# First projection of a two-layer decoder trunk: four row groups, sums seeded into the accumulators, spatial loads a block ahead

## The chip, the cores and the metric

The kernel runs on one core of one Trainium2 chip. The metric is the device time of one execution in microseconds; lower is better. A run's time is the span from the first to the last instruction plus a little around it.

## The reference

A two-layer decoder trunk works on one sequence of 256 tokens with width 2048, all in float32. Each layer takes a conditioning vector c, makes six sections of modulation from it (adaLN), and runs a mixer and a SwiGLU feed-forward (FFN), each behind a modulated RMS norm. The change lies in layer 0, in the projection that feeds its mixer, and in its FFN:

```python
mod = (silu(c) @ ada_w[layer] + ada_b[layer])[:, None, :]
sh_m, sc_m, g_m, sh_f, sc_f, g_f = jnp.split(mod, 6, axis=-1)
hm = rms_norm(x, norm_mix_g[layer]) * (1.0 + sc_m) + sh_m
proj = jnp.einsum('bsd,de->bse', hm, w_in)              # (256, 2048) by (2048, 10272)
u, v, z, xbc, dt_raw = jnp.split(proj, ...)
y_a = chunked_spatial_gating(gelu(u), gelu(v), gm_ln_g, gm_ln_b, gm_w_s, gm_b_s)
y_b = ssd_mixer(z, xbc, dt_raw, ...)                    # conv + silu on xbc, scan, norm, times silu(z)
x = x + (1.0 + g_m) * (concat([y_a, y_b]) @ w_out)
x = x + (1.0 + g_f) * ((silu(hf @ w_gate) * (hf @ w_up)) @ w_down)
```

`chunked_spatial_gating` normalises v over its channels, scales it with gm_ln_g and gm_ln_b, and mixes tokens with a causal 128 by 128 matrix for each of 16 heads (gm_w_s).

## The kernel before

**Products.** A float32 product is made of three products of parts: each operand is split into a high and a low part, and hi by h, lo by h and hi by l are summed. A weight slab of 512 columns and two row tiles (256 of the 2048 input channels) is loaded by SP as `raw` (four buffers), rounded by ScalarE into `hi` (L330, three buffers), and the rest `lo` is made by VectorE (L335, three buffers). `wslab` records these three. An input row tile k is the pair `h`, `l`: ScalarE makes h from the normalised x and the modulation (L529), VectorE makes l (L530).

**Blocks and accumulators.** The projection is done in blocks of 512 output columns, 14 of them in the part that the change touches, in the order of `ORDER`: x (the convolution's input, transposed), v and z. x and z blocks come from `dense_ws`, whose weight is the moving operand (12 products of 256 columns for each row tile), v blocks from `dense_as` (6 products of 512 columns for each row tile). A block's sum stands in one of two PSUM accumulators of 128x1024 (`psA`, named accps). The pool gives a block the accumulator that was released first, in the order in which the program asks for them.

**Row groups.** The contraction cannot run over all 16 row tiles at once, since each row tile needs its piece of sh_m and sc_m, and these come from ada_w (a stream of `araw` loads, accumulated on VectorE at L205 and L207, then transposed on PE at L153, reduced at L220, added to the bias at L224). So `grouped` splits the 16 row tiles into `GROUPS`, here of 4, 5 and 7. For each group it runs all 14 blocks over the group's row tiles. After the first group, ScalarE copies the accumulator into an SBUF buffer (L584). In the later groups VectorE adds the accumulator to that buffer (L586). While a group runs, the modulation of the next (a `group_unit`) is loaded and accumulated in the background; `RATES` says how many such steps are put between slabs, `LAGS` how late their VectorE part follows. The first group has no cover: `opening` waits for its modulation, loaded right after x, with some matmuls on the landed tiles that only keep PE warm (`firsts`).

**Last group.** After a block of the last group, `finish0` takes its full sum from the SBUF buffer: convolution and silu for x, gelu with a running sum for v (L987), silu for z (L990). After the tenth block comes the LayerNorm of v, and at the blocks in `GM_AT` one quarter of v is normalised (L952) and mixed (L960, L962), with the loads of gm_ln_g, gm_ln_b and gm_w_s issued at that place.

**Order.** A scheduling layer sets the order of each engine from the order of recording and from priorities (`high_priority`, `issue_after`). Each engine then runs its list in that order, and waits on semaphores.

The FFN of layer 0 uses the same `grouped` with two groups of eight row tiles (`FGROUPS`) and 12 blocks.

Of the kernel before, what the change touches and what calls it, by code (L numbers as in the profile page):

```python
# [39 lines left out]
FIRST_A = (7, 8, 9)  # L40
SMALLS_AT = 4
QUIET = 8
RATES = (1.3, 0.92, 0.0)
RATE = 0.75
# [4 lines left out]
LN_AT = 9  # L49
GM_AT = (9, 11, 12, 13)  # L50
SSD_AT = (12, 14, 18, 20)
# [3 lines left out]
def trunk(ctx: ExitStack, tc: tile.TileContext, x, c, norm_mix_g, norm_ffn_g, ada_w, ada_b,  # L55
# [59 lines left out]
    first_rows = {8: lambda: nc.sync.dma_start(rows3[0:96, :], ada_b[0].rearrange("(k p) -> k p", p=P)),  # L115
                  9: lambda: nc.sync.dma_start(rows3[96:128, :], norm_mix_g.rearrange("l (k p) -> (l k) p", p=P))}

# [72 lines left out]
    def ada_unit(layer, base, stride, width, dst, nr=2):  # L190
# [18 lines left out]
        def end():  # L209
            n = width // P  # L210
            if nr == 1:
                first_mod.append(acc)
                return
            total = tmp.tile([P, 32], F32, tag="tot", name="tot", bufs=2)[:, 0:nr * n]
# [12 lines left out]
            if dst[0][0] in (2, 5):  # L227
                gate_to_rows(layer, dst[0][0])

        for g0 in range(0, KT * nr, nk):  # L230
            raw = (bt() if nr == 1 and g0 not in FIRST_A else
                   adp.tile([P, 1024], F32, tag="araw", name="araw", bufs=A_BUFS))
            for i in range(nk):
# [143 lines left out]

    def dense_ws(w, c0, ks, ahead=W_AHEAD):

        acc = psA.tile([P, 1024], F32, tag="acc", name="accps").rearrange("p (n t) -> p n t", n=4)  # L380
        done = 0
        for run in slabs(ks):
# [12 lines left out]
            for n, (a, b, first, final) in order:  # L395
                dense_mm[0] = T.matmul(acc[:, n, :], a[:, n * P:(n + 1) * P], b, start=first and n % 2 == 0,  # L396
                                       stop=final, skip_group_check=True)
# [18 lines left out]

    def dense_as(w, c0, ks, ahead=W_AHEAD, head=None, tail=False, hold=False):

        if tail:
            accs = [pm(), pm()]
        else:
            full = psA.tile([P, 1024], F32, tag="acc", name="accps").rearrange("p (n t) -> p n t", n=2)
            accs = [full[:, 0, :], full[:, 1, :]]
# [5 lines left out]
        for pi, part in enumerate(parts):  # L431
# [15 lines left out]
            for n, j, (r, i, x) in order:  # L447
# [7 lines left out]
                def product(n=n, j=j, i=i, x=x, bh=bh, bl=bl, hi=hi, lo=lo, last=pi == len(parts) - 1):  # L455
                    return mm(accs[n], (bl if x == 1 else bh)[:, n * P:(n + 1) * P], (lo if x == 2 else hi)[:, i, :],
                              first=pi == 0 and j == 0, last=last and j == len(ops) - 1)

# [88 lines left out]

    def grouped(blocks, groups, layer, sh, make, finish, rates, lags, heads=None, early=0):

# [3 lines left out]
        def begin(gi):  # L553
# [6 lines left out]
            hs.extend(make(k0, kg))  # L560

        for gi, (k0, kg) in enumerate(groups):
            if not (early and gi):
# [4 lines left out]
            for i, (dense, w, c0, dst) in enumerate(blocks):  # L568
                if early and not last and i == len(blocks) - early:
                    begin(gi + 1)  # L570
                args = {"head": heads} if heads and gi == 0 and i == 0 else {}
                if not ks:
# [5 lines left out]
                if dst is None:  # L578
                    if gi == 0:
                        fdst.append(tb())  # L580
                    dst = fdst[i]
                with tc.high_priority(offset=600):
                    if gi == 0:
                        A.activation(dst, acc, AF.Copy)  # L584
                    else:
                        V.tensor_tensor(dst, acc, dst, op=OP.add)  # L586
                if last:
                    finish(i)
                if gi == 0 and sh == 0 and i == 10:
                    later_cols()  # L590
# [5 lines left out]
    with tc.high_priority(offset=50000):  # L596
# [40 lines left out]
        with tc.issue_after(last.ins):  # L637
            psw = pm()
            for t in firsts[10:]:
                mm(psw, ident, t)  # L640
        take()

    def opening(w, c0, n):
# [67 lines left out]

        acc = psA.tile([P, 1024], F32, tag="acc", name="accps").rearrange("p (n t) -> p n t", n=4)

# [219 lines left out]
    def layer_norm():  # L933
# [9 lines left out]
        V.reciprocal(rv, rv)  # L943

    def layer_norm_apply(b):
        gB = t2()
        nc.sync.dma_start(gB, gm_ln_g[:, 512 * b:512 * (b + 1)].partition_broadcast(P))
        bB = t2()
        nc.sync.dma_start(bB, gm_ln_b[:, 512 * b:512 * (b + 1)].partition_broadcast(P))
        for cc in range(2):  # L950
# [4 lines left out]
    def spatial(b):  # L955
        wraw = t2().rearrange("p (h s) -> p h s", h=4)
        nc.sync.dma_start(wraw, gm_w_s[0, 4 * b:4 * b + 4].rearrange("h t s -> t h s"))
        ps = pm()
        for h in range(4):
            T.transpose(ps[:, h * P:(h + 1) * P], wraw[:, h, :], ident)  # L960
        w = t2().rearrange("p (h t) -> p h t", h=4)
# [15 lines left out]

    def finish0(i):
        kind, j = (ORDER[i][0], int(ORDER[i][1])) if i < len(ORDER) else ("", 0)
# [4 lines left out]
        elif kind == "v":  # L984
            t = vt[j]
            for cc in range(2):
                A.activation(t[:, cc, :], t[:, cc, :], AF.Gelu_apprx_tanh, accum_out=sums[:, cc, j:j + 1])  # L987
        elif kind == "z":
            with tc.high_priority(offset=600):
                A.activation(zb[j], zb[j], AF.Silu)  # L990
# [312 lines left out]

    def finishf(i):
        t = fdst[i]
        with tc.high_priority(offset=600):
            if i % 2 == 0:
                A.activation(t, t, AF.Silu)
            else:
                sg = fdst[i - 1]  # L1310
                V.tensor_tensor(sg, t, sg, op=OP.mult)
                ffn_split(sg, 4 * (i // 2), a)

    hf = grouped(fblocks, FGROUPS, 0, 3, makef, finishf, F_RATES, (LAGS[-1], LAGS[-1]), normf.head, 2)
    ffn_in(0, hf, 4 * FPAIRS, 6 - FPAIRS, a)
# [197 lines left out]
```

## Time and profile before

| | us |
|---|---|
| median of 3 runs | 2564.55 |
| lowest, highest | 2564.42, 2566.23 |
| profiled execution, its time | 2565.73 |
| its span, first to last instruction | 2563.9 |
| PE busy in the span | 2528.8 |
| VectorE (DVE) busy | 1862.2 |
| ScalarE (ACT) busy | 1265.6 |
| first product of the first block | 37.79 |
| first product of the second group | 121.69 |

The profile is one execution. The engines are PE (matmul), PEld (its weight loads), DVE (VectorE), ACT (ScalarE), POOL (GpSimd) and SP (which issues most DMAs). A row of a timeline has the start, the duration, the engine, the line in the kernel, the operation, and output and input by their names; what stands in brackets is the idle time before it and what ended that. A group row has the count, then the busy time, the mean in nanoseconds and the idle time. A windows row has, for each engine, the busy time and count, then the clock that PE was granted (1.00 is full speed), the share of time that the DMA engines were busy, and what they moved in GB/s. The projection up to the end of its last group takes the first 393 us.

### The profile page before, as it was taken

How to read it: one execution, taken by the hardware profiler on the slowest of the kernel's cores; microseconds unless marked ns; L12 is line 12 of the kernel's file. 1: busy time of each engine (PE TensorE's matmuls, PEld its weight loads, DVE VectorE, ACT ScalarE, POOL GpSimd, SP SyncE). 2: the span in 40 equal slices, each digit the busy share in tenths (PEclk: the TensorE clock that was granted, in tenths of full speed). 3: DMA queues.
4: the chain of work that ended last, by engine and by line, in shares of the span. 5: the costliest groups of instructions: out<-in, count | busy, mean ns of one | idle time of the engine just before them, and what ended most of it. 6: DMA issues, size and time to landing. Idle time of an engine off the chain costs nothing.

```text
span 2563.9 us, 33519 instructions
## 1 busy us (share of the span) xinstructions
PE 2528.8 (99%) x12485; PEld 2128.0 (83%) x12485; DVE 1862.2 (73%) x1993; ACT 1265.6 (49%) x1640; POOL 6.5 (0%) x19
## 2 busy tenths in 40 slices
PE   7999989999999999999999999999999999999999
PEld 6999888878788888888888788888788888888887
DVE  6799888899878888777777777677764455545454
ACT  5534766555545444344444665554744443344443
POOL 0000000000000000000000000000000000000000
PEclk9999999999999999999999999999999999999999
DMA  8999668998799989999988688878676656666664
GB/s 325 321 343 328 185 202 259 309 318 297 264 326 329 314 302 310 325 316 302 302 308 304 223 282 261 272 263 282 197 257 196 192 189 200 204 190 189 188 204 166
DMA packets 309630, 676.01 MB, mean 264 GB/s; under 512 B 24272, under 2 KB 26842, under 8 KB 309466
## 3 DMA queue, kind: packets, MB, share of 16 engines
q1 hardware_dynamic: 309338, 673.85, 79.2%
q8 instruction: 98, 1.61, 0.2%
q14 instruction: 66, 0.54, 0.1%
q10 hardware_dynamic: 128, 0.02, 0.0%
HBM read 671.62 MB, written 2.16 MB: 263 GB/s over the span
## 4 chain that ended last, share of the span: by engine, by line
PE 96%; DVE 1%; DMA 1%; ACT 1%; issue 0%; SPq 0%; DVEq 0%; ACTq 0%
PE accps L162 79%; PE accps L396 8%; PE pm L162 6%; PE pm L153 2%; DMA t<-in_gm_w_s 1%; DVE acc L207 0%; DMA blk<-in_ada_w 0%; ACT hi L330 0%; DVE lo L335 0%; DMA raw<-in_ffn_w_gate 0%; DVE t L867 0%; PE pm L887 0%; ACT t L939 0%; DVE t L1145 0%; ACT h L1141 0%
## 5 line engine op out<-in xcount | busy, mean ns | idle before, releaser
L330 ACT ACTIVATE hi<-raw 128x1024 fp32r<-128x1024 f32 (+1 forms) x864 | 903.6, 1047 | 1177.1 <-PE accps L162 1016.8
L335 DVE TENSOR_TENSOR lo<-raw,hi 128x1024 fp32r<-128x1024 f32 (+1 forms) x864 | 1040.3, 1206 | 578.1 <-ACT hi L330 571.4
L162 PE MATMUL accps<-hi,h 128*128 128x512 f32 x2224 | 603.8, 392 | 0.0
L162 PE MATMUL accps<-lo,h 128*128 128x512 f32 x2224 | 600.4, 391 | 0.0
L162 PE MATMUL accps<-hi,l 128*128 128x512 f32 x2224 | 599.9, 390 | 0.0
L162 PEld LDWEIGHTS accps<-hi,l 128*128 128x128 f32 x2224 | 416.5, 188 | 87.1 <-issue 0.8
L162 PEld LDWEIGHTS accps<-lo,h 128*128 128x128 f32 x2224 | 415.4, 188 | 87.1 <-issue 1.6
L162 PEld LDWEIGHTS accps<-hi,h 128*128 128x128 f32 x2224 | 412.6, 188 | 83.3 <-issue 0.6
L207 DVE SCALAR_TENSOR_TENSOR acc<-araw,ct,acc 128x1024 f32<-128x1024 f32 (+2 forms) x377 | 465.3, 1234 | 2.7 <-DMA araw<-in_ada_w 2.0
L162 PE MATMUL accps<-hi,blk 128*128 128x512 f32 x1440 | 357.4, 390 | 0.0
L162 PEld LDWEIGHTS accps<-hi,blk 128*128 128x128 f32 x1440 | 269.5, 188 | 55.5
L162 PE MATMUL accps<-lo,blk 128*128 128x512 f32 x720 | 192.6, 389 | 0.0
L396 PE MATMUL accps<-h,lo 128*128 128x256 f32 x624 | 164.0, 287 | 3.1 <-DVE lo L335 3.1
L396 PE MATMUL accps<-h,hi 128*128 128x256 f32 x624 | 163.7, 286 | 2.3 <-ACT h L529 1.7
L396 PE MATMUL accps<-l,hi 128*128 128x256 f32 x624 | 163.2, 286 | 0.4 <-DVE l L530 0.4
L162 PEld LDWEIGHTS accps<-lo,blk 128*128 128x128 f32 x720 | 135.1, 188 | 28.0
L396 PEld LDWEIGHTS accps<-h,hi 128*128 128x128 f32 x624 | 115.2, 193 | 4.5 <-ACT h L529 1.9
L396 PEld LDWEIGHTS accps<-h,lo 128*128 128x128 f32 x624 | 114.7, 194 | 4.7 <-DVE lo L335 3.5
L396 PEld LDWEIGHTS accps<-l,hi 128*128 128x128 f32 x624 | 115.0, 195 | 0.8 <-DVE l L530 0.6
L162 PE MATMUL pm<-hi,blk 128*128 128x512 f32 x224 | 57.0, 390 | 0.6 <-ACT hi L330 0.6
L586 DVE TENSOR_TENSOR blk<-accps,blk 128x1024 f32<-128x1024 f32 x40 | 48.7, 1218 | 3.8 <-PE accps L162 2.6
L162 PEld LDWEIGHTS pm<-hi,blk 128*128 128x128 f32 x224 | 42.0, 188 | 9.8 <-ACT hi L330 1.1
(277 smaller groups left out, 1319.4 us busy)
## 6 DMA issues: line engine op xcount, KB each, us to landing
araw<-in_ada_w SPq DMA_DIRECT2D x323, 512.0 KB, 5.6
raw<-in_ffn_w_gate SPq DMA_DIRECT2D x176, 512.0 KB, 4.5
raw<-in_ffn_w_up SPq DMA_DIRECT2D x176, 512.0 KB, 4.5
raw<-in_ffn_w_down SPq DMA_DIRECT2D x176, 512.0 KB, 4.4
raw<-in_ab_w_in SPq DMA_DIRECT2D x128, 512.0 KB, 5.0
raw<-in_cd_w_in SPq DMA_DIRECT2D x96, 512.0 KB, 4.7
raw<-in_ab_w_out SPq DMA_DIRECT2D x64, 512.0 KB, 5.5
raw<-in_cd_w_out SPq DMA_DIRECT2D x32, 512.0 KB, 5.0
```

Source lines behind the costliest of these rows:

```text
L153: return T.transpose(dst, src, ident)
L162: return T.matmul(o, a, b, start=first, stop=last, skip_group_check=True)
L207: V.scalar_tensor_tensor(acc, r, ct[nr][:, g:g + 1], acc, op0=OP.mult, op1=OP.add)
L330: A.activation(hi, raw, AF.Copy)
L335: wlast[1] = V.tensor_tensor(lo, raw, hi.bitcast(F32), op=OP.subtract)
L396: dense_mm[0] = T.matmul(acc[:, n, :], a[:, n * P:(n + 1) * P], b, start=first and n % 2 == 0, stop=final, skip_group_check=True)
L586: V.tensor_tensor(dst, acc, dst, op=OP.add)
```

## The change

There are three edits. First, `GROUPS` becomes four groups of 2, 3, 5 and 6 row tiles. Second, in the inner groups, and for v and z blocks of the last group, ScalarE writes a block's running sum into the accumulator before the block's first product (in the rows below: `accps<-blk`, a seed; its block's products then only add). The copy-out after a block is then ScalarE's in all groups but the last, and `finish0` reads v and z straight out of the accumulator. x blocks of the last group still start from zero and are added by VectorE. A function `reserve` takes the accumulators of the present block and of the next one. Third, `load_gm` issues the LayerNorm and spatial loads of a quarter one block before they are used, into tiles of their own. The same seeds serve the FFN of layer 0, where both kinds of block are read from the accumulator. Lines in the changed kernel stand up to some 40 lower or higher than before (hi L328, lo L333, seed L580, copy-out L610, h L531, gelu L1022).

```diff
-GROUPS = ((0, 4), (4, 5), (9, 7))
+GROUPS = ((0, 2), (2, 3), (5, 5), (10, 6))
-LAGS = (2, 4, 6)
+LAGS = (2, 2, 4, 6)
-RATES = (1.3, 0.92, 0.0)
+RATES = (1.3, 1.3, 0.92, 0.0)
-GM_AT = (9, 11, 12, 13)
+GM_AT = (9, 11, 13, 15)
...
-                dense_mm[0] = T.matmul(acc[:, n, :], a[:, n * P:(n + 1) * P], b, start=first and n % 2 == 0,
+                dense_mm[0] = T.matmul(acc[:, n, :], a[:, n * P:(n + 1) * P], b, start=first and n % 2 == 0 and not seeded,
...
+        def seeded(gi, i):
+            return gi > 0 and (gi < len(groups) - 1 or direct(i))
+
+        def reserve(at):
+
+            n = order.index(at)
+            for gi, i in order[n:n + 2]:
+                if (gi, i) not in accs:
+                    accs[gi, i] = acc_tile()
+                    if seeded(gi, i):
+                        dst = blocks[i][3] if blocks[i][3] is not None else fdst[i]
+                        with tc.high_priority(offset=600):
+                            A.activation(accs[gi, i], dst.rearrange("p n t -> p (n t)"), AF.Copy)
+            return {"into": accs[at], "seeded": seeded(*at)}
...
+                if last and direct(i):
+                    finish(i, acc)
+                    continue
                 with tc.high_priority(offset=600):
-                    if gi == 0:
+                    if not last:
                         A.activation(dst, acc, AF.Copy)
                     else:
                         V.tensor_tensor(dst, acc, dst, op=OP.add)
...
-            for t in firsts[10:]:
+            for t in firsts[4:]:
...
+    def load_gm(b):
+        t = gm_loads[b] = [tmp.tile([P, 512], F32, tag="gate", name="gm", bufs=2) for _ in range(2)]
+        t += [tmp.tile([P, S], F32, tag="wg", name="wg", bufs=1), hp.tile([P, S], F32, tag="l%d" % KT, name="wg")]
+        with tc.issue_after(wlast[0].ins):
+            nc.sync.dma_start(t[0], gm_ln_g[:, 512 * b:512 * (b + 1)].partition_broadcast(P))
...
-            for cc in range(2):
-                A.activation(t[:, cc, :], t[:, cc, :], AF.Gelu_apprx_tanh, accum_out=sums[:, cc, j:j + 1])
+            with tc.high_priority(offset=600):
+                for cc in range(2):
+                    A.activation(t[:, cc, :], acc[:, cc, :], AF.Gelu_apprx_tanh, accum_out=sums[:, cc, j:j + 1])
         elif kind == "z":
             with tc.high_priority(offset=600):
-                A.activation(zb[j], zb[j], AF.Silu)
+                A.activation(zb[j], acc, AF.Silu)
...
         for b in range(4):
+            if GM_AT[b] == i + 1:
+                load_gm(b)
...
-    grouped(blocks0, GROUPS, 0, 0, make0, finish0, RATES, LAGS)
+    grouped(blocks0, GROUPS, 0, 0, make0, finish0, RATES, LAGS, lambda i: ORDER[i][0] != "x")
```

How the change stands on the engines is shown at three places. The numbers behind the names are those of the tiles.

The first is ScalarE in the last group, from the slabs of block x5 (the third of `ORDER`) to the gelu of v0 (the second) and beyond. Before:

```order
L330 ACTIVATE hi_2842<-raw_2840 128x1024
L330 ACTIVATE hi_2872<-raw_2870 128x1024
L821 ACTIVATE t2_2584<-t2_2584 128x64
L822 ACTIVATE t2_2584<-t2_2584 128x64
L330 ACTIVATE hi_2902<-raw_2900 128x1024
L330 ACTIVATE hi_2932<-raw_2930 128x512
L987 ACT_TABLE_LOAD
L987 ACTIVATE blk_316,sums_330<-blk_316 128x512 x2
L330 ACTIVATE hi_2976<-raw_2974 128x1024
```

Now (accps_2988 is v0's accumulator, accps_3166 that of v1, the fourth block; hi_3170, 3200 and 3230 are x5's slabs):

```order
L328 ACTIVATE hi_3170<-raw_3168 128x1024
L580 ACTIVATE accps_3166<-blk_307 128x1024
L328 ACTIVATE hi_3200<-raw_3198 128x1024
L328 ACTIVATE hi_3230<-raw_3228 128x1024
L1022 ACT_TABLE_LOAD
L1022 ACTIVATE blk_306,sums_320<-accps_2988 128x512 x2
L328 ACTIVATE hi_3286<-raw_3284 128x1024
```

The gelu, which read and wrote an SBUF buffer behind VectorE's add, now reads the accumulator; the seed of v1 has come in two slabs ahead of it. The accumulator of x5 between them, accps_3106, has the same PSUM address as accps_2988, and its first product waits for the second gelu. The same holds for the blocks behind v1, v2, v3 and z0.

The second is PE around the end of the first group. Before (h_431 is group 0's last row tile, h_1323 group 1's first):

```order
L396 MATMUL accps<-l_432,hi 128x256
L153 MATMUL pm<-ident,acc 128x128 x5
L396 MATMUL accps<-h_431,lo 128x256
L396 MATMUL accps<-h_431,hi 128x256
...
L396 MATMUL accps<-h_431,lo 128x256
L396 MATMUL accps<-h_1323,hi 128x256 x4
L396 MATMUL accps<-h_1323,lo 128x256 x4
```

Now (h_368 is group 0's last, h_876 and h_882 group 1's first two; the L161 rows are block v0's):

```order
L398 MATMUL accps<-h_368,lo 128x256
L152 MATMUL pm<-ident,acc 128x128 x3
L398 MATMUL accps<-h_876,hi 128x256 x4
L398 MATMUL accps<-h_876,lo 128x256 x4
L161 MATMUL accps<-hi,h_876 128x512 x2
L161 MATMUL accps<-hi,h_882 128x512 x2
L398 MATMUL accps<-l_877,hi 128x256 x4
```

The transposes of the next group's modulation stood ten products before the group's end and stand behind its last product now. Products of the second block have come in between those of the first.

The third is ScalarE behind that place, in the first three blocks of group 1 (accps_836, accps_892 and accps_952 in turn; hi_956 is the second block's slab, hi_1067 the fourth's):

```order
L531 ACTIVATE h3_882<-xs3_230,mod0_0_113,gs_0_1_2_872 128x256
L328 ACTIVATE hi_930<-raw_928 128x512
L328 ACTIVATE hi_956<-raw_954 128x1024
L531 ACTIVATE h4_888<-xs4_237,mod0_0_113,gs_0_1_2_872 128x256
L328 ACTIVATE hi_977<-raw_975 128x512
L328 ACTIVATE hi_996<-raw_994 128x1024
L328 ACTIVATE hi_1031<-raw_1029 128x512
L610 ACTIVATE blk_304<-accps_836 128x1024
L328 ACTIVATE hi_1067<-raw_1065 128x1024
L610 ACTIVATE blk_306<-accps_892 128x1024
L580 ACTIVATE accps_952<-blk_305 128x1024
```

The copy-outs L610 and the seed L580 are new in this group, where VectorE's add L586 stood; the third block's seed stands behind the fourth block's hi and the second block's copy-out.

More of the change, by code (lines that the diff above doesn't have):

```diff
@@ L213, in end @@
                 return
[L214 removed]
+            total = t1()[:, 0:nr * n]
             for j0 in range(0, n, 4):
@@ L230, in ada_unit @@
         for g0 in range(0, KT * nr, nk):
-            raw = (bt() if nr == 1 and g0 not in FIRST_A else
-                   adp.tile([P, 1024], F32, tag="araw", name="araw", bufs=A_BUFS))
+            raw = bt() if nr == 1 else adp.tile([P, 1024], F32, tag="araw", name="araw", bufs=A_BUFS)
             for i in range(nk):
@@ L376, in queue_turns, with acc_tile, dense_ws @@
             preps.append(lambda j=j: turn(j, src[j // 2], make))
-    def dense_ws(w, c0, ks, ahead=W_AHEAD):
-        acc = psA.tile([P, 1024], F32, tag="acc", name="accps").rearrange("p (n t) -> p n t", n=4)
+    def acc_tile():
+        return psA.tile([P, 1024], F32, tag="acc", name="accps")
+    def dense_ws(w, c0, ks, ahead=W_AHEAD, into=None, seeded=False):
+        acc = (into or acc_tile()).rearrange("p (n t) -> p n t", n=4)
         done = 0
@@ L415, in run_held, with dense_as @@
                 dense_mm[0] = held.pop(0)()
-    def dense_as(w, c0, ks, ahead=W_AHEAD, head=None, tail=False, hold=False):
+    def dense_as(w, c0, ks, ahead=W_AHEAD, head=None, tail=False, hold=False, into=None, seeded=False):
         if tail:
@@ L423, in dense_as @@
         else:
-            full = psA.tile([P, 1024], F32, tag="acc", name="accps").rearrange("p (n t) -> p n t", n=2)
+            full = (into or acc_tile()).rearrange("p (n t) -> p n t", n=2)
             accs = [full[:, 0, :], full[:, 1, :]]
@@ L456, in product @@
                     return mm(accs[n], (bl if x == 1 else bh)[:, n * P:(n + 1) * P], (lo if x == 2 else hi)[:, i, :],
-                              first=pi == 0 and j == 0, last=last and j == len(ops) - 1)
+                              first=pi == 0 and j == 0 and not seeded, last=last and j == len(ops) - 1)
                 if hold and len(part) > 1 and n == 1 and j >= len(ops) - 2:
@@ L546, in trunk, with grouped @@
     fdst = []
-    def grouped(blocks, groups, layer, sh, make, finish, rates, lags, heads=None, early=0):
+    def grouped(blocks, groups, layer, sh, make, finish, rates, lags, direct, heads=None, early=0):
         hs = []
@@ L560, in begin @@
             hs.extend(make(k0, kg))
+        order = [(gi, i) for gi in range(len(groups)) for i in range(len(blocks))]
+        accs = {}
+        def seeded(gi, i):
[10 more added lines that the diff above has]
+            return {"into": accs[at], "seeded": seeded(*at)}
         for gi, (k0, kg) in enumerate(groups):
@@ L570, in grouped @@
                     begin(gi + 1)
-                args = {"head": heads} if heads and gi == 0 and i == 0 else {}
+                args = reserve((gi, i)) if ks else {}
+                if heads and gi == 0 and i == 0:
+                    args["head"] = heads
                 if not ks:
@@ L588, in grouped @@
                     finish(i)
-                if gi == 0 and sh == 0 and i == 10:
+                if gi == 1 and sh == 0 and i == 2:
                     later_cols()
@@ L710, in rest @@
                 run("V", lambda: V.scalar_tensor_tensor(h[k][1], xs[k], g[k], t, op0=OP.mult, op1=OP.subtract))
-        acc = psA.tile([P, 1024], F32, tag="acc", name="accps").rearrange("p (n t) -> p n t", n=4)
+        acc = acc_tile().rearrange("p (n t) -> p n t", n=4)
         def products(k):
@@ L943, in layer_norm @@
         V.reciprocal(rv, rv)
+    gm_loads = {}
+    def load_gm(b):
[3 more added lines that the diff above has]
+            nc.sync.dma_start(t[0], gm_ln_g[:, 512 * b:512 * (b + 1)].partition_broadcast(P))
+            nc.sync.dma_start(t[1], gm_ln_b[:, 512 * b:512 * (b + 1)].partition_broadcast(P))
+            for i in range(2):
+                nc.sync.dma_start(t[2 + i].rearrange("p (h s) -> p h s", h=2),
+                                  gm_w_s[0, 4 * b + 2 * i:4 * b + 2 * i + 2].rearrange("h t s -> t h s"))
     def layer_norm_apply(b):
[L946 to L949, printed above, removed]
+        gB, bB = gm_loads[b][0:2]
         for cc in range(2):
@@ L976, in ssd_out, with finish0 @@
             ssqy.add(zb[g][:, j, :])
-    def finish0(i):
+    def finish0(i, acc=None):
         kind, j = (ORDER[i][0], int(ORDER[i][1])) if i < len(ORDER) else ("", 0)
```

20 lines of the change are left out of this document (9 added, 11 removed).

## The prediction

> **What bounds the kernel now.** I read the page's head and chain first, then a table of windows over the stage that the change touches, then the timelines at its seams. Page: the span, the engines' busy time, the chain by engine.
>
> ```profile
> span 2563.9 us, 33519 instructions
> PE 2528.8 (99%) x12485; PEld 2128.0 (83%) x12485; DVE 1862.2 (73%) x1993; ACT 1265.6 (49%) x1640; POOL 6.5 (0%) x19
> PE 96%; DVE 1%; DMA 1%; ACT 1%; issue 0%; SPq 0%; DVEq 0%; ACTq 0%
> ```
>
> PE is the bound: 35.1 us of the span (2563.9 - 2528.8) are not matmul. The change removes no dense product, so it can only move those 35 us, or the time lost to a lower clock, which counts as busy. Windows (busy per engine, then PE clock, DMA share, GB/s):
>
> ```profile
> 10.00:30.00 20.00, 14.40 (x75) 11.56 (x75) 16.30 (x18) 8.34 (x24) 0.00 (x0) 1.00 1.05 406
> 35.00:40.00 5.00, 5.00 (x25) 5.00 (x25) 2.48 (x10) 1.97 (x4) 0.00 (x0) 0.50 0.42 117
> 120.00:122.00 2.00, 0.31 (x2) 0.31 (x3) 1.91 (x3) 1.98 (x3) 0.00 (x0) 1.00 0.95 379
> 124.00:126.00 2.00, 2.00 (x11) 2.00 (x11) 2.00 (x5) 1.08 (x3) 0.00 (x0) 0.50 0.72 260
> 130.00:222.00 92.00, 92.00 (x662) 87.18 (x661) 87.26 (x90) 38.06 (x43) 0.00 (x0) 1.00 0.97 340
> 222.00:393.00 171.00, 163.70 (x1187) 152.62 (x1186) 145.39 (x232) 115.82 (x192) 0.00 (x0) 0.99 0.72 223
> 330.00:333.00 3.00, 3.00 (x28) 3.00 (x27) 2.55 (x6) 1.79 (x5) 0.00 (x0) 1.00 0.87 295
> 339.00:342.00 3.00, 3.00 (x16) 3.00 (x16) 3.00 (x5) 0.47 (x2) 0.00 (x0) 0.52 0.76 208
> 393.00:2560.00 2167.00, 2162.75 (x9912) 1786.66 (x9910) 1532.05 (x1554) 1044.06 (x1300) 4.95 (x6) 1.00 0.79 261
> ```
>
> After 393 us PE idles 4.3 us in 2167: nothing to win there. In 130 to 222 DVE is 95% busy and DMA share 0.97, yet PE never waits, so relieving DVE there is worth nothing. What can move is the opening, the seams between groups, and the last group (222 to 393), which idles 7.3 us. PE's waits in that window, PE's timeline at the opening and the first seam, and two pieces of the chain:
>
> ```profile
> PE pm L960 <- DMA t<-in_gm_w_s: 3.6, 2, 2.3
> PE accps L396 <- DVE lo L335: 3.1, 2, 2.4
> ```
> ```profile
> 25.45 3.82 PE L162 MATMUL pm<-blk,ident 128*128 128x512 f32 x8
> 34.53 3.50 PE L162 MATMUL pm<-ones,acc 128*128 128x64 f32 x16 [2.63 <-DVE acc L207]
> 37.79 1.20 PE L162 MATMUL accps<-h,hi 128*128 128x256 f32 x4
> 45.26 1.09 PE L162 MATMUL accps<-hi,h 128*128 128x512 f32 x4
> 118.06 0.71 PE L153 MATMUL pm<-ident,acc 128*128 128x128 f32 x5
> 121.69 0.74 PE L396 MATMUL accps<-h,hi 128*128 128x256 f32 x4 [1.74 <-ACT h L529]
> 123.28 1.11 PE L396 MATMUL accps<-l,hi 128*128 128x256 f32 x4 [0.37 <-DVE l L530]
> ```
> ```profile
> 3.12 8.06 DMA blk<-in_ada_w
> 62.11 5.75 PE accps L396 x48
> ```
>
> Durations for the sum, from the groups of 0 to 400 us:
>
> ```profile
> L330 ACT ACTIVATE hi<-raw 128x1024 fp32r<-128x1024 f32 x101 | 106.7, 1058 | 117.8 <-PE accps L396 70.4 <-PE accps L162 26.8 <-DMA raw<-in_ab_w_in 13.5
> L584 ACT ACTIVATE blk<-accps 128x1024 f32<-128x1024 f32 x14 | 14.1, 1010 | 7.5 <-PE accps L396 4.4 <-PE accps L162 3.1
> L586 DVE TENSOR_TENSOR blk<-accps,blk 128x1024 f32<-128x1024 f32 x28 | 34.1, 1217 | 0.7 <-PE accps L396 0.7
> L207 DVE SCALAR_TENSOR_TENSOR acc<-araw,ct,acc 128x640 f32<-128x640 f32 x31 | 27.3, 881 | 1.3 <-DMA araw<-in_ada_w 1.0
> L207 DVE SCALAR_TENSOR_TENSOR acc<-araw,ct,acc 128x1024 f32<-128x1024 f32 x17 | 21.6, 1273 | 0.1
> L987 ACT ACTIVATE blk<-blk 128x512 f32<-128x512 f32 x8 | 5.0, 625 | 0.7 <-DVE blk L586 0.7
> L987 ACT ACT_TABLE_LOAD x3 | 3.8, 1283 | 0.1
> L990 ACT ACTIVATE blk<-blk 128x1024 f32<-128x1024 f32 x3 | 3.1, 1049 | 1.0 <-DVE blk L586 1.0
> L529 ACT ACTIVATE h<-xs,mod,gs 128x256 fp32r<-128x256 f32 x12 | 6.3, 588 | 0.0
> ```
>
> **The change, part by part.** *Opening.* Two row tiles instead of four halve the first adaLN accumulation: 16 updates of 512 columns instead of 16 of 1024, and 4.2 MB instead of 8.4 MB at the 406 GB/s of 10 to 30 us (10 us less of loading). From 0.881 at 640 columns and 1.273 at 1024, one of 512 takes about 0.75; the first data lands at 11.2, so DVE, with its small steps between, ends near 26. PE's own work is then last: at 25.45 its earlier products are done, eight warming matmuls (3.82, the row of 25.45) end at 29.3, the sums halve (3.50/2 = 1.75), so the first product starts near 30.9, 6.9 earlier than 37.79. There is no 2.63 us hole before it, so the half clock of 35 to 40 goes too. The first block took 45.26 - 37.79 = 7.47 us; twelve-matmul blocks later take 5.75 for 48 matmuls (0.12 each), so 1.7 were lost. **-8.6.**
>
> *Spatial loads a block ahead.* The 3.6 us on the spatial weights go, and so do the 3.1 us on lo, which stands on DVE behind the LayerNorm step that waits for its own loads. The 1.4 us of clock lost in 339 to 342 (3 us at 0.52) and 0.3 around it go with them. On SP the loads now stand among the weight slabs of the block before, 0.77 MB (three of 256 KB) in some 9 us at DMA share 0.72, in one issue more per block since the spatial weights come in halves: free. **-8.4.**
>
> *Seam 0 to 1.* In the order, unit 1's transposes stand behind all of group 0's products; before, ten products followed them. The chain of 118.06 to 121.69 (3.63 us: transposes, reduce, two updates of mod, gs, h) becomes about 3.6 after the last product, since a three-row reduce is shorter but one more update of 640 columns stands ahead of mod. Then block 1's hi stands on ACT behind both h and one other hi (0.59 + 0.6 for half a slab + 1.06, against 0.96 us of products): 1.1 more. Block 2's seed stands behind a hi that needs the end of block 1, and behind block 1's copy-out: from 0.5 before block 1's end, 1.06 + 1.01 + 1.05 (seed) + 0.1, so 2.7. Sum 7.4 against some 2.8 idle now (3.63 less ten products at 0.12, plus the 0.37 ahead of 123.28): **+4.6.** Bounds: 0, if PE's queue absorbs both, and +8, if DMA cannot hold the pace of group 0.
>
> *The seed's price* is not in the trace. ACT moving 1024 columns costs 1.010 out of the accumulator and 1.058 between buffers; I take 1.05, range 1.0 to 1.1. It removes a DVE add of 1.217 in 22 of 28 blocks, worth nothing, since DVE ends no wait there.
>
> *Seams 1 to 2 and 2 to 3, and seeds inside group 1.* Per three-row block ACT now has 1.06 + 0.63 + 1.01 + 1.05 = 3.75 of 4.3 us (36 products at 0.12). At the next seam five h (0.588 each) and the seed follow a copy-out on ACT, and the first product waits for the seed: an estimate of +1.5, since half of that queue already stands there today; six h at the last: +0.7; seeds that stand behind a hi inside the group: +0.9. **+3.1** (0 to 6). Group 0's last block gets the same accumulator as the one before it, and waits for the copy-out: **+1.1.**
>
> *Last group.* This carries the sum. Before, blocks alternated between two accumulators, so an epilogue always had a block's time. Now the seed of the next v or z block takes the free one early, and the x block between gets the accumulator that the v block has just left. It cannot start until both gelus have read it. On ACT ahead of them stands the x block's third hi, whose buffer the v block's last slab holds. Timeline of ACT and PE at such a place now:
>
> ```profile
> 268.22 0.62 PE L162 MATMUL accps<-hi,l 128*128 128x512 f32 x2
> 269.13 0.64 PE L396 MATMUL accps<-h,hi 128*128 128x256 f32 x4
> ```
> ```profile
> 268.88 1.06 ACT L330 ACTIVATE hi<-raw 128x1024 fp32r<-128x1024 f32 x1 [0.75 <-PE accps L162]
> 270.65 0.63 ACT L987 ACTIVATE blk<-blk 128x512 f32<-128x512 f32 x1 [0.71 <-DVE blk L586]
> 271.28 0.61 ACT L987 ACTIVATE blk<-blk 128x512 f32<-128x512 f32 x1
> 280.30 1.28 ACT L840 ACT_TABLE_LOAD   x1
> 281.59 0.23 ACT L840 ACTIVATE dte<-dte 128x32 f32<-128x32 f32 x1
> ```
>
> hi begins when the last hi-by-l product ends (268.84). With a two-row last slab, four more products of 0.23 follow, so the next block would start 0.7 after that. From there hi 1.06, table load 1.28, gelus 0.63 + 0.61, and 0.1 for the accumulators' read-out: 3.7. PE stands 3.7 - 0.7 = 3.0, four times: 12.0. The block after z0 waits likewise for hi and silu, 1.06 + 1.05 + 0.2 = 2.3. Behind the gelus on ACT stand the hi of the block after and the convolution's steps; they have a block's time and are not late. **+14.3** (10 if the hi or the load is early, 16 if the hi is late by half its time each).
>
> Here a rule bears. In the rows, 280.30 + 1.28 runs straight into the next instruction at 281.59, so a switch costs 1.28. The Trainium skill, "ScalarE: Activation LUTs", section "What ACT_TABLE_LOAD costs", adds a drain of about 1380 ns to every switch; by it the four places would cost an estimated 5.5 more. The trace shows none, and the sum goes by the trace.
>
> *Clock.* After 1.7 us of idle in 120 to 122 PE ran at 0.50 in 124 to 126; after 2.3 us in 327 to 330 it kept 1.00. So each new stall of 2.7 to 3.0 us costs 0 to 1.7 more; half, five times: **+4.2.** The Trainium skill, "TensorE: Matmul & The Clock Gate", section "What's actually happening", halves the clock after an idle window of about 3.4 us; by it 3.0 us stalls cost nothing here. The trace has the loss after less idle, so I keep the half.
>
> *FFN.* Same edit in two groups. DVE adds (12) become seeds; PE has no wait there to remove. The last block of its first group shares an accumulator and waits for one copy-out: **+1.1.**
>
> Sum: -8.6 - 8.4 + 4.6 + 3.1 + 1.1 + 14.3 + 4.2 + 1.1 = +11.4. The profiled execution took 2565.73, 1.83 around its span and 1.2 above the median of the three runs, so 2577.1 against it, and 2576 as a median.
>
> **Rivals.** *Faster:* ACT runs ahead of where I put it, so that its hi, table load and seeds are done when PE needs them, and only what needs a finished sum stays on the path. For it: ACT is busy 68% of 222 to 393 (115.82 of 171) and 41% of 130 to 222. Against: the hi ahead of the gelus needs a buffer that the v block holds almost to its end. Then the gelu pair costs 1.3, four times 5.2, silu 1.1, the clock nothing, group 1's seeds and block 2's wait nothing: 11.4 - 8.0 - 4.2 - 3.1 - 2.7 = -6.6, so 2558. It decides where the last group's waits stay under 2 us each.
>
> *No change:* the gelu waits come as forecast, but the clock holds and PE's queue fills the first seam: 11.4 - 4.2 - 4.6 = +2.6, so 2567.
>
> *DMA-bound:* groups 0 to 2 now load ten row tiles of weights (14 blocks of 0.26 MB each, 36.7 MB), adaLN for all 16 (4.2 + 29.4), 16 steps of later sections (8.4) and x (2.1): 81 MB by the start of the last group near 243 us, 333 GB/s on average. The trace held 340 at share 0.97 in 130 to 222 without a stall, and 406 at the opening. If 340 is the ceiling with the opening's slow start, 0 to 10 us more: up to 2586.
>
> **How the numbers follow.** A difference under 0.2% (5.1 us) is no change here. Forecast as summed 0.5, DMA-bound 0.2, no change 0.18, faster 0.12. Below 2559.4: 0.12; within: 0.18; above 2569.7: 0.70. Low end 2560: clock 0, seams at their low bounds. High end 2593: DMA 10, clock and seams at their high bounds in part. The range is set by the clock (0 to 8), the seams (0 to 14) and the gelu waits (10 to 16).
>
> **What would show it.** Right: the first product near 31 us at clock 1.0; no wait on in_gm_w_s; five waits of accps for the gelu or silu in the last group, 2 to 3 us each, and a clock below 1 after them; one wait of the third block of group 1 for the seed; the last group ending near 405. Wrong: no wait on gelu, which removes 14 us; or waits on raw<-in_ab_w_in in the first 240 us, which would mean DMA.

## The result, and the profile after

The changed kernel takes 2590.97 us (median of 4 runs, 2588.35 to 2593.67) against 2564.49 us before (2564.17 to 2566.23): a ratio of 1.0103, 95% interval 1.0087 to 1.0119. It is slower, by 26.5 us where 11.4 were forecast. The profiled execution is the fastest of the four, 2588.35 us, and that of before (2565.73) one of its slower ones, so the traces compare at +22.6 and can't show where the other 3.9 us of the 26.5 lie. Each experiment below is given as its median, then the ratio to the kernel before with its 95% interval. All medians of the experiments below stand beside runs of the kernel before on the same chip, which gave 2563.2 to 2564.0.

The page of the changed kernel, the lines that answer to those shown of before:

```profile
span 2586.6 us, 33665 instructions
...
PE 2529.8 (98%) x12475; PEld 2127.1 (82%) x12475; DVE 1833.3 (71%) x1995; ACT 1343.6 (52%) x1720; POOL 4.9 (0%) x19
...
PE 84%; ACT 2%; DMA 1%; DVE 1%; issue 0%; SPq 0%; ACTq 0%; DVEq 0%
```

PE's busy time is the same within 1 us (2528.8 before). So 21.7 of the 22.7 us of span are idle time of PE (time at a low clock counts as busy). VectorE has lost 29 us of work, ScalarE has gained 78. PE's waits, the largest, of the whole span (total, times, longest in us; left out are those of the opening that stood in the kernel before too):

```profile
PE accps L398 <- ACT blk L1022: 11.7, 4, 4.7
...
PE accps L398 <- ACT accps L580: 5.3, 3, 3.3
...
PE accps L398 <- ACT h L531: 3.3, 1, 3.3
PE accps L398 <- ACT blk L1025: 2.8, 1, 2.8
...
PE accps L398 <- DVE lo L333: 2.4, 4, 1.0
PE pm L152 <- DVE acc L206: 2.2, 1, 2.2
...
PE pm L161 <- DVE t L937: 1.8, 1, 1.8
PE accps L398 <- ACT blk L610: 1.1, 1, 1.1
```

L1022 is the gelu, L1025 the silu, L580 the seed. PE's timeline shows where they fall: the first product, the seam from group 0 to 1, the third block of group 1, group 2's first, the start of the last group (250.43), its five waits, and its end:

```profile
29.74 0.74 PE L161 MATMUL accps<-h,hi 128*128 128x256 f32 x4 [0.69 <-ACT h L725]
...
67.99 0.74 PE L398 MATMUL accps<-h,hi 128*128 128x256 f32 x4 [1.11 <-ACT blk L610]
...
73.31 0.55 PE L152 MATMUL pm<-ident,acc 128*128 128x128 f32 x3 [2.19 <-DVE acc L206]
...
77.21 1.22 PE L398 MATMUL accps<-h,hi 128*128 128x256 f32 x4 [3.35 <-ACT h L531]
...
90.88 1.22 PE L398 MATMUL accps<-h,hi 128*128 128x256 f32 x4 [3.29 <-ACT accps L580]
...
148.03 0.74 PE L398 MATMUL accps<-h,hi 128*128 128x256 f32 x4 [1.71 <-ACT accps L580]
...
250.43 0.28 PE L156 MATMUL pm<-h,t 128*32 128x256 f32 x1
...
276.11 0.73 PE L398 MATMUL accps<-h,hi 128*128 128x256 f32 x4 [2.82 <-ACT blk L1022]
...
299.20 1.22 PE L398 MATMUL accps<-h,hi 128*128 128x256 f32 x4 [4.70 <-ACT blk L1022]
...
320.54 0.74 PE L398 MATMUL accps<-h,hi 128*128 128x256 f32 x4 [2.82 <-ACT blk L1022]
...
340.44 1.22 PE L398 MATMUL accps<-h,hi 128*128 128x256 f32 x4 [1.31 <-ACT blk L1022]
...
362.09 0.74 PE L398 MATMUL accps<-h,hi 128*128 128x256 f32 x4 [2.80 <-ACT blk L1025]
...
414.71 1.17 PE L161 MATMUL accps<-hi,h 128*128 128x512 f32 x4
```

Of before, the start and the end of the last group:

```profile
222.74 0.28 PE L157 MATMUL pm<-h,t 128*32 128x256 f32 x1
...
393.11 1.08 PE L162 MATMUL accps<-hi,h 128*128 128x512 f32 x4
```

The stage ends 21.6 us later (414.71 - 393.11), so nearly all is lost before 415 us. A row tile of the 14 blocks takes 19.8 us (10 times 12 products at 0.12, 4 times 6 at 0.227). The last group has one row tile less, so it would have started at 222.74 + 19.8 = 242.5 with the old losses. It starts at 250.43: the regrouping has cost 7.9 by then, though the first product is 8.05 earlier. The last group takes 164.3 us; 170.4 - 19.8 = 150.6 would be the old figure, so it has lost 13.7. The five waits are 14.5 us. PE's other waits there, for the scan's outputs most of all, are 4.0 us, where all waits of the last group were 7.3 before; a lower clock (0.97 for 0.99) is most of the rest. What stands behind the last group adds 1.1 us (0.7 of them the wait in the FFN for a copy-out, forecast as 1.1).

ScalarE ahead of the first of the five waits reads as it was foreseen:

```profile
272.41 1.06 ACT L328 ACTIVATE hi<-raw 128x1024 fp32r<-128x1024 f32 x1 [1.61 <-PE accps L161]
273.49 1.28 ACT L1022 ACT_TABLE_LOAD   x1
274.79 0.60 ACT L1022 ACTIVATE blk<-accps 128x512 f32<-128x512 f32 x1
...
275.37 0.59 ACT L1022 ACTIVATE blk<-accps 128x512 f32<-128x512 f32 x1
```

hi, table load, two gelus, and PE goes on at 276.11. Ahead of the second of them (4.70, PE idle from 294.50) the convolution's steps of the block before, with a table load of their own, stand ahead of that hi:

```profile
291.36 1.28 ACT L895 ACT_TABLE_LOAD   x1
...
294.24 1.07 ACT L890 ACTIVATE t<-blk,cols 128x256 f32<-128x256 f32 x2
...
295.52 1.04 ACT L328 ACTIVATE hi<-raw 128x1024 fp32r<-128x1024 f32 x1
```

### The profile page after: what moved, and what is told of

It reads as the page before. It is cut to its first block, busy times and chain, and to the rows that moved or that the text cites. A ratio compares the mean times of both kernels' runs of the same rounds, so it can differ in the third digit from the quotient of the medians.

```text
span 2586.6 us, 33665 instructions
## 1 busy us (share of the span) xinstructions
PE 2529.8 (98%) x12475; PEld 2127.1 (82%) x12475; DVE 1833.3 (71%) x1995; ACT 1343.6 (52%) x1720; POOL 4.9 (0%) x19
## 4 chain that ended last, share of the span: by engine, by line
PE 84%; ACT 2%; DMA 1%; DVE 1%; issue 0%; SPq 0%; ACTq 0%; DVEq 0%
PE accps L161 75%; PE pm L161 5%; PE pm L152 2%; PE accps L398 1%; ACT hi L328 0%; DMA wg<-in_gm_w_s 0%; DVE lo L333 0%; ACT L895 0%; DMA raw<-in_ffn_w_gate 0%; ACT t L934 0%; DMA raw<-in_ab_w_in 0%; DMA raw<-in_cd_w_in 0%; ACT L941 0%; DVE t L1182 0%; ACT h L1178 0%
## 5 line engine op out<-in xcount | busy, mean ns | idle before, releaser
L328 ACT ACTIVATE hi<-raw 128x1024 fp32r<-128x1024 f32 (+1 forms) x865 | 903.4, 1046 | 1131.4 <-PE accps L161 986.5
L333 DVE TENSOR_TENSOR lo<-raw,hi 128x1024 fp32r<-128x1024 f32 (+1 forms) x865 | 1040.5, 1205 | 588.7 <-ACT hi L328 584.6
L161 PE MATMUL accps<-hi,h 128*128 128x512 f32 x2224 | 604.5, 393 | 0.7 <-ACT blk L610 0.7
L161 PE MATMUL accps<-hi,l 128*128 128x512 f32 x2224 | 600.0, 390 | 0.0
L161 PE MATMUL accps<-lo,h 128*128 128x512 f32 x2224 | 599.8, 391 | 0.0
L206 DVE SCALAR_TENSOR_TENSOR acc<-araw,ct,acc 128x1024 f32<-128x1024 f32 (+3 forms) x405 | 476.5, 1176 | 27.9 <-DMA araw<-in_ada_w 26.8
L161 PEld LDWEIGHTS accps<-lo,h 128*128 128x128 f32 x2224 | 416.2, 188 | 87.6 <-issue 1.6
L161 PEld LDWEIGHTS accps<-hi,l 128*128 128x128 f32 x2224 | 416.3, 188 | 87.1 <-issue 0.8
L161 PEld LDWEIGHTS accps<-hi,h 128*128 128x128 f32 x2224 | 412.6, 188 | 84.0 <-ACT blk L610 0.9
L161 PE MATMUL accps<-hi,blk 128*128 128x512 f32 x1440 | 357.2, 390 | 0.0
L161 PEld LDWEIGHTS accps<-hi,blk 128*128 128x128 f32 x1440 | 269.5, 188 | 55.5
L161 PE MATMUL accps<-lo,blk 128*128 128x512 f32 x720 | 192.7, 389 | 0.0
L398 PE MATMUL accps<-h,hi 128*128 128x256 f32 x632 | 164.0, 290 | 24.4 <-ACT blk L1022 11.7
L161 PEld LDWEIGHTS accps<-lo,blk 128*128 128x128 f32 x720 | 135.1, 188 | 28.0
L610 ACT ACTIVATE blk<-accps 128x1024 f32<-128x1024 f32 x54 | 54.6, 1011 | 6.7 <-PE accps L398 4.7
L161 PE MATMUL pm<-hi,blk 128*128 128x512 f32 x224 | 57.0, 390 | 0.3 <-ACT hi L328 0.3
L580 ACT ACTIVATE accps<-blk 128x1024 f32<-128x1024 f32 x48 | 49.1, 1024 | 6.3 <-DVE blk L1347 5.5
```

The source lines that it names most:

```text
L161: return T.matmul(o, a, b, start=first, stop=last, skip_group_check=True)
L206: V.scalar_tensor_tensor(acc, r, ct[nr][:, g:g + 1], acc, op0=OP.mult, op1=OP.add)
L328: A.activation(hi, raw, AF.Copy)
L333: wlast[1] = V.tensor_tensor(lo, raw, hi.bitcast(F32), op=OP.subtract)
L580: A.activation(accs[gi, i], dst.rearrange("p n t -> p (n t)"), AF.Copy)
```

## Experiments

**Accumulators that alternate (e1).** In the last group, the edit holds the next block's claim on an accumulator, and with it its seed, until the present block has started (shortened; the comments are added):

```diff
-                    accs[gi, i] = acc_tile()      # and its seed, at once
+                    if sh == 0 and at[0] == len(groups) - 1 and (gi, i) != at:
+                        at_start.append(lambda gi=gi, i=i: take_acc(gi, i))   # run behind the first product
```

> The changed kernel, but in the last group of the projection the seed of the next block is held back until the present block has started, so that blocks alternate between the two accumulators again. Theory (the accumulator): the five waits for gelu and silu in the last group (11.7 + 2.8 us) and 2 to 4 us of low clock behind them go, so some 17 us below the changed kernel, about 2574. Rival (ScalarE is the bound there, and the wait moves from the gelu to the late seed): the wait returns as one of accps for the seed, and under 5 us are won, above 2585.

Measured: 2571.92 us, 1.0039 of before (1.0024 to 1.0054). PE's waits in 240 to 415 us, the whole list:

```profile
PE accps L404 <- DVE lo L333: 3.9, 3, 2.0
PE pm L1010 <- DMA wg<-in_gm_w_s: 1.9, 1, 1.9
PE accps L161 <- ACT hi L328: 1.1, 1, 1.1
```

The five waits are gone, and with them 17.8 us of the loss (26.5 less 8.7). No wait for a seed has come in their place. The theory holds. In the traces the win is 16.6 us: 14.5 of the five waits, less 2.9 by which the others there have grown (4.0 to 6.9), and the clock, which is 1.00 in 250 to 415 us for 0.97 (some 4 us of 146.5 busy).

**Last group unseeded (e2).** `direct` is false for every block, and gelu and silu read the SBUF buffers behind VectorE's add.

> The changed kernel without seeds in the last group of the projection: VectorE adds there, and gelu and silu work in SBUF as before. The inner groups and the FFN keep their seeds. Theory (the accumulator): the five waits go as in the run above, about 2574, within 4 us of it, since neither the seed nor the add is on the path. Rival (VectorE's adds cost what the seeds had saved): over 5 us slower than the run above.

Measured: 2572.37 us, 1.0041 (1.0026 to 1.0055), the same as e1. Reading the accumulator directly gains nothing over the add; what hurt was the accumulator that both blocks share.

**No seeds in the projection (e3).** As e2, and `seeded` is false in the inner groups.

> As the run above, and without seeds in the inner groups too: VectorE adds in all of the projection's later groups. Groups of 2, 3, 5 and 6 and the spatial loads a block ahead stay, and the FFN's seeds. Theory (seeds queued on ScalarE cost the seams): the waits of accps for the seed (3.3 + 1.7 + 0.3 us) and the half clock of 75 to 90 us behind the first of them go, 8 to 12 us below the run above, about 2564. Rival (the seams cost that because a group of two or three row tiles is too short for the modulation of the next): the waits stay under other names, within 4 us of the run above.

Measured: 2579.50 us, 1.0069 (1.0052 to 1.0086): 7 us slower than e2. The theory falls; the rival's mechanism is what the trace shows, at more than the 4 us it allowed. PE's waits in 24 to 260 us, the largest:

```profile
PE pm L152 <- DVE acc L206: 9.7, 2, 8.0
PE accps L398 <- ACT h L531: 6.7, 2, 4.4
...
```

The waits for the seed are gone, but the transposes at the seam from group 1 to 2 stand 8.0 us for VectorE. In a group of three row tiles, 14 adds of 1.217 us are 17 us that VectorE does not have beside the next group's modulation. So the seeds do pay where a group is short, if all its blocks would else be added (for four of them see e6).

**The early loads alone (e4),** on the kernel before: `load_gm` and `GM_AT` of the change, nothing else but one small buffer moved to make room. `GM_AT` also puts the last two uses two blocks later.

> The kernel before with one edit alone: the LayerNorm and spatial loads a block ahead, with the later places of use. Theory: the 6.7 us of PE waits on these loads and about 1.7 us of low clock go, so 8 us below the kernel before, 2556. Rival (what stands behind them is late anyway: the scan's outputs at the end of the group, which are waited for in the changed kernel): 2 to 4 us, 2561.

Measured: 2562.97 us (10 runs), 1.0002 (0.9992 to 1.0011): nothing won. PE's waits in the last group, all of them:

```profile
PE accps L396 <- ACT hi L330: 5.6, 4, 3.6
PE accps L396 <- DVE lo L335: 0.8, 1, 0.8
```

The theory falls, and so do the rival's 2 to 4 us, though something else was late, as it said. Of the 7.3 us of waits before, the 3.6 on the loads are gone and lo's 3.1 are 0.8, but hi's have grown from 0.6 to 5.6, and the low clock has only moved (0.72 in 371 to 377 us, for 0.52 in 339 to 342). ScalarE is in the scan's exponentials there, with a hi behind each of several table loads. Its timeline ahead of the longest of these waits, where PE goes on at 370.62:

```profile
364.37 1.28 ACT L998 ACT_TABLE_LOAD   x1
365.67 1.06 ACT L998 ACTIVATE blk<-blk 128x1024 f32<-128x1024 f32 x1
366.63 1.26 ACT L908 ACTIVATE t<-bc,atk 128x128 f32<-128x128 f32 x4
367.91 1.28 ACT L915 ACT_TABLE_LOAD   x1
369.20 0.42 ACT L915 ACTIVATE t<-bc 128x256 f32<-128x256 f32 x1
369.53 1.04 ACT L330 ACTIVATE hi<-raw 128x1024 fp32r<-128x1024 f32 x1
```

**The old groups (e5):** e1 with 4, 5 and 7 row tiles and the old opening; seeds and early loads stay.

> The kernel of the first experiment (accumulators alternate) with the row groups of before (4, 5 and 7) and its opening: seeds and early loads stay. Theory (the four groups are the rest of the loss: the opening wins some 10 us and the seams lose 17): the wait of accps for the seed in the second group's third block and the late modulation go, and the time is within 3 us of the kernel before. Rival (the seeds themselves cost ScalarE's time everywhere): it stays 6 to 9 us above the kernel before, as the first experiment did.

Measured: 2563.95 us (10 runs), 1.0003 (0.9994 to 1.0013). The theory holds: what e1 still loses, 8 us, belongs to the four groups. Seeds and early loads together win nothing in three long groups that shows beside some 2.5 us of noise.

**Four blocks of group 1 added by VectorE (e6):** `seeded` is false for `gi == 1 and i < 4`.

> The kernel of the first experiment, with the first four blocks of group 1 unseeded and added by VectorE. Theory (the seed of the third block is queued behind a copy-out and a hi, and PE's 3.8 us of idle there also halves the clock): 4 to 7 us below the first experiment, about 2 to 5 above the kernel before. Rival (VectorE is what group 1 lacks: four adds of 1.2 us make the next modulation late): the wait moves to the transposes at the next seam, and the time is the first experiment's within 2 us, or above.

Measured: 2570.71 us, 1.0034 (1.0021 to 1.0047), within 2 us of e1, as the rival said; its mechanism does not show, since the transposes at the next seam wait for nothing. There PE waits 2.7 us for h, where e1 waits 1.8 for a seed. The third block's wait for the seed (3.80 in e1) became one of 2.77 for VectorE's add:

```profile
88.76 0.81 PE L404 MATMUL accps<-h,hi 128*128 128x256 f32 x4 [2.77 <-DVE blk L628]
```

**Half of group 0's weights not loaded (e7,** shortened):

```diff
-            wlast[0] = nc.sync.dma_start(rk, w[k0 * P:(k0 + nk) * P, c0:c0 + ncol].rearrange(...))
+            wlast[0] = nc.sync.dma_start(raw[:, 0:ncol], w[k0 * P:(k0 + 1) * P, c0:c0 + ncol])   # in group 0
```

> The kernel of the first experiment, but in group 0 each weight slab after the first block loads only its first row tile, and ScalarE and VectorE read that half twice; so the second row tile is multiplied with the first one's weights. All engines work as before; 3.4 of some 14 MB in 30 to 75 us aren't loaded. Theory (DMA is full in group 0, so the modulation of group 1 is late): VectorE's waits for araw in 45 to 77 us (5.4 us) fall under 2, the transposes start at once, and 2 to 5 us are won with the clock. Rival (the chain behind the transposes and the seeds set the seam, DMA only fills the time): under 1.5 us.

Measured: 2571.84 us, 1.0039 (1.0025 to 1.0053), no gain. The transposes no longer wait, and the gap behind them has grown from 4.52 in e1 to:

```profile
76.23 1.22 PE L410 MATMUL accps<-h,hi 128*128 128x256 f32 x4 [4.69 <-ACT h L547]
```

Group 1 starts 1.2 us earlier than in e1 (77.47). VectorE's waits for araw in its updates (L206) in 30 to 80 us fell from 5.4 to 3.0 us, not under 2. So the load of group 0's weights is not what sets this seam. One wait for a load does stand in its chain, in e7 as in e1: 1.4 us for the next unit's first araw, ahead of group 1's modulation (see e12).

**Three groups of 3, 5 and 8 (e8):** `GROUPS`, `LAGS` and `RATES` alone.

> The kernel of the first experiment with three groups of 3, 5 and 8 row tiles. Theory (each seam of a short group costs 5 to 8 us, and a first group of 3 keeps half of the opening's 10): 5 us below the first experiment, within 4 us of the kernel before. Rival (DMA: groups of 3 and 5 must load the modulation of 5 and 8 at 355 GB/s and more): the transposes at both seams wait 5 us or more for VectorE, and the time is the first experiment's or above.

Measured: 2576.28 us, 1.0056 (1.0041 to 1.0071): above the first experiment, as the rival said, though its sign holds in part only: the transposes wait 3.40 us at the first seam and not at the second. PE at its seam from group 0 to 1:

```profile
106.18 0.76 PE L152 MATMUL pm<-ident,acc 128*128 128x128 f32 x5 [3.40 <-DVE acc L206]
113.39 1.01 PE L404 MATMUL accps<-h,hi 128*128 128x256 f32 x3 [6.44 <-ACT h L541]
```

VectorE waits 17 us for araw in 30 to 115 us. Here fewer seams did not help, with a next group 1.67 times as large.

**PE kept warm at the seam (e9):** four unused matmuls behind the transposes.

> The kernel of the first experiment with four more matmuls of 128x512 (0.48 us each half, some 3.8 us in all) on PE at the first seam, behind the transposes of group 1's modulation; their result isn't used. They fill the idle time before group 1's first product (4.5 us) and move nothing else. Theory (part of the seam's price is the clock: 0.81 in 75 to 90 us): group 1's first product starts at the same time within 0.5 us, the clock of 75 to 90 us rises to 0.95 or more, and 2 to 4 us are won. Rival (the clock follows the later wait for the seed, or the extra matmuls push the first product): within 1 us of the first experiment.

Measured: 2571.97 us, 1.0034 (1.0022 to 1.0047): the rival. The clock of 75 to 90 us is 1.00 where e1 had 0.81, and the third block still starts at 91.03 (91.54 in e1; 1.3 us sooner if counted from the first product, 30.55 here and 29.75 in e1), behind its seed:

```profile
75.00:90.00 15.00, 11.26 (x60) 8.29 (x58) 13.34 (x24) 8.20 (x12) 0.00 (x0) 1.00 0.83 253
91.03 0.74 PE L405 MATMUL accps<-h,hi 128*128 128x256 f32 x4 [3.90 <-ACT accps L595]
```

At this seam a lower clock mostly fills time that PE would wait.

**A scan step moved out of the last group (e10, e11):** `SSD_AT = (14, 16, 18, 20)` for `(12, 14, 18, 20)`, on e4 and on e5. The second step moves with the first.

> The kernel before with the loads a block ahead, as in the fourth experiment, and with the first of the scan's four output steps two blocks later, behind the projection's last group, where PE never waits. Theory (the waits on the loads were replaced by waits for hi, since ScalarE stands in the scan's exponentials and table loads): the waits for hi (5.6 us) fall under 2.5, and the time is 3 to 5 us below the fourth experiment and the kernel before. Rival (the next in line is VectorE's lo or the scan's chain itself): the waits return under those names, within 1.5 us of the fourth experiment.

> The same later scan step in the kernel of the fifth experiment (groups of 4, 5 and 7, seeds with alternating accumulators, early loads). Theory: as above, 3 to 5 us below the fifth experiment, and level with the run above if the seeds are worth nothing where groups are long. Rival (the seeds free VectorE, which is next in line): 2 us or more below the run above.

Measured: e10 2566.89 us, 1.0013 (1.0004 to 1.0022); e11 2575.81 us, 1.0052 (1.0039 to 1.0064): both slower than what they were built on. In e10 the waits for hi in the last group did fall to 1.4 us, which bears out the reading of e4, but another has come at 500 to 520 us:

```profile
PE accps L162 <- ACT h L486: 5.0, 2, 3.4
```

All of the last group's waits together fell from 6.4 to 3.2 us, and this wait takes back 5.0, with the low clock that e4 had at 360 to 380 (0.91) now at 500 to 520. That is 1.8 of the 3.2 us by which e10 is behind e4. e11 is 11 us behind e5, each against its own runs of before. In its trace, that of its slowest run, the waits in 500 to 520 are 6.0 us at a clock of 0.84 (2.2 us more), and those of the last group 8.5 us, for 5.3 in e5 with the seam ahead of it; most of that is a wait for the spatial weights (3.2 for 0.5). Together this is about what it loses; why the weights came late there is open.

**The modulation first (e12):** in e1, VectorE's first two steps for group 2 stand behind group 1's modulation (`take` stops behind `end`, and goes on after the first l).

> The kernel of the first experiment with two steps on VectorE moved: at the first seam the first two steps of group 2's modulation (one waits 1.4 us for its load, the other takes 0.88) stand behind group 1's modulation and first l, not ahead of them. Theory (the chain from the transposes to the first product sets the seam): the gap ahead of group 1's first product falls from 4.5 to some 2.5 us, all later seams keep their place, and 2 to 3 us are won, near 2569.5 where the kernel before takes 2563.5. Rival (the seam is set by ScalarE's queue up to the third block's seed): the third block starts where it started, its wait grows by what the first product has gained, and under 1 us is won.

Measured: 2569.66 us (10 runs), 1.0025 (1.0016 to 1.0035). The seam in its trace:

```profile
72.31 0.55 PE L152 MATMUL pm<-ident,acc 128*128 128x128 f32 x3 [0.20 <-DVE acc L206]
...
74.81 0.74 PE L408 MATMUL accps<-h,hi 128*128 128x256 f32 x4 [1.95 <-ACT h L545]
...
87.91 0.74 PE L408 MATMUL accps<-h,hi 128*128 128x256 f32 x4 [2.90 <-ACT accps L595]
```

The gap is 1.95 for 4.52, and the third block starts 3.6 us earlier than in e1. In the time it is 2.3 us between medians, with intervals that overlap, so the trace shows the theory at this seam and the time only agrees. The last group starts 3.6 us earlier too (248.42 for 251.99); there a wait of 3.5 us for lo, and a clock of 0.53 behind it in 345 to 350 us, take part of that back. None of the versions beats the kernel before.

## Why the prediction was right or wrong

- *The direction and the main mechanism were right.* The last group's five waits were put at 14.3 us; the trace has 11.7 + 2.8 = 14.5. With the clock behind the four gelus (3.4 forecast) the term was 17.7, and e1 won back 17.8.
- *The size of the five waits was right by luck.* Its 3.0 for a gelu should have been 2.8, which is what two of the four measure (2.82): four more products of 0.23 are 0.9 and not 0.7, and PE would have gone on 0.9 behind the start of hi (273.29 and 272.41). What failed is the sentence that the convolution's steps "have a block's time and are not late". They made the second wait 4.70. At z0 a table load of theirs (358.47) stands ahead of hi (360.09), and the wait is 2.80 where 2.3 was forecast, and 1.4 with the same 0.9 taken off. The fourth wait is only 1.31, since the transposes of the spatial weights and a wait for them fill the first half of it. In e1's trace the other waits grew by 2.9 us, so its 17.8 is not the price of the five waits and the clock behind them alone.
- *The step that failed most: "Spatial loads a block ahead", -8.4.* The waits on the loads nearly went (0.7 us is left), but e4 shows that they were the last of several late things: with them gone, hi was late by nearly as much. The prediction named what the loads had blocked, and not what would be late next; it gave the term no range. The term is 0 in e4 (within 2.5 us), an error of 8.4. In the changed kernel, what was late next were the scan's outputs: the last group's waits other than the five are 4.0 us where 0.6 were left by the forecast.
- *The step that failed second: the regrouping, mis-sized.* Opening (-8.6), seam 0 to 1 (+4.6), seams and seeds (+3.1), the shared accumulator at the end of group 0 (+1.1) and a share of the clock (+0.8) sum to +1.0. e1 less e5 is 8.7 - 0.8 = 7.9, with 4 to 5 us to either side, and so says the trace. The opening won more than forecast (the first product 8.05 earlier for 6.9, and the 1.7 of clock). The seam terms were too small, by some 8 us. The chain from group 0's last product to group 1's first was put at 3.6 us; it is 6.1, since the transposes waited 2.19 for VectorE, which was not ready as assumed, and the next unit's steps stood in the chain (e12). The third block's wait is 3.29 for 2.7, the one at 148.03 is 1.71 for 1.5; behind 100 us PE waits 4.1 us in all for seeds and lo, where 3.1 were forecast. The clock of 60 to 100 us is 0.87 (3.9 us of 30.05 busy), where before lost some 1.5 at its seam and 0.8 more was forecast. The wait of block 1's hi (1.1, by its own terms 1.3) did not come. Together that is 4 to 5 of the 8 us; where the rest lies the trace does not show.
- *The seed's price was right, its worth was wrong.* It took 1.022 us where 1.05 was taken. But "worth nothing, since DVE ends no wait there" was read from groups of 4 and 5; with none in the groups of three and five, e3 loses 7 us net, and its one long wait (8.0) is at the end of the group of three. With four of that group's blocks added by VectorE (e6) nothing is lost.
- *The clock: right in size for the wrong stalls.* Windows behind three of the five waits of the last group:

```profile
276.00:282.00 6.00, 5.89 (x49) 5.90 (x50) 2.81 (x9) 1.11 (x2) 0.00 (x0) 1.00 0.29 89
...
299.00:305.00 6.00, 5.80 (x36) 5.81 (x37) 1.89 (x6) 3.15 (x7) 0.00 (x0) 0.72 0.30 87
...
340.00:346.00 6.00, 5.55 (x35) 5.56 (x36) 1.69 (x5) 5.97 (x16) 0.00 (x0) 0.72 0.57 188
```

After 2.82 us of idle the clock held, and it held after the other two of 2.8; after 4.70, and after 0.68 and 1.31 close together, 1.7 us were lost (6 us at 0.72). So two in five lost it. Outside of the five it was 0.67 in 405 to 410, behind the scan's waits, which no term had. The Trainium skill, "TensorE: Matmul & The Clock Gate", section "What's actually happening", says that the clock halves after an idle window of about 3.4 us. The four single waits agree with it, the two short ones at 340 do not. The table load costs what it did in the rows of before: 273.49 + 1.28 runs into 274.79. The Trainium skill, "ScalarE: Activation LUTs", section "What ACT_TABLE_LOAD costs", adds a drain of about 1380 ns. The trace shows none.
- *DMA-bound* (0.2) was not the cause in group 0: e7 took away a quarter of its transfers and gained nothing. For the groups behind it that is argued and not tested. Its sign is there: ScalarE waits 12.9 us for raw<-in_ab_w_in in 30 to 250 us, but it did so before too (14.5 in 38 to 222), and VectorE's waits for araw are 28 us where they were 1.5. What reaches PE of it is bounded by PE's waits, 4.1 us in all from 100 to 250 us.
- The sum: 11.4, and 8.4 and 6.9 more from the two failed steps, is 26.7; 26.5 was measured. That it closes proves little, since the steps are differences between runs in a chain from 26.5 to 0 (e1, then e5). The time lies inside the range (2560 to 2593), but not for the range's reasons: its high end was built from 10 us of DMA, the clock and the seams, and the loads had no part in it. The last group was to end near 405 and ended at 414.71.

## What to carry to other kernels

Writing the next block's start into an accumulator early also claims the accumulator early. With two of them, check which block shares with which before asking what the write costs, and claim in the order of use. A wait that ends last hides the others: price its removal by what is late next on each engine, not by its own length.

## What was not expected of the hardware

Only the clock: PE's granted clock of 0.81 over 15 us at the first seam cost nothing that the time shows (e9), and waits of 2.8 us left it at 1.00 three times, where 0.68 + 1.31 us close together lowered it to 0.72.
